# HGRN2 within a chunk: a tree of block totals, with keys and queries scaled in place level by level

## The chip, the cores and the metric

The kernel runs on one core of one Trainium2 chip. The metric is the device time of one execution in microseconds, the median of the runs; lower is better. The core has five engines that run side by side, each with an instruction queue of its own that it works through in order: PE (matrix products), DVE (elementwise work on vectors), ACT (functions such as the exponential), POOL (a second, more general elementwise engine) and SP (which here issues the DMAs).

## The reference

The reference is a two-layer decoder trunk on 512 tokens of width 1024. Layer 0 is attention, layer 1 a recurrent mixer (a Mamba-2 group and an HGRN2 group), each followed by a gated feed-forward part; a norm ends it. The change touches the HGRN2 group alone, four heads with 128 keys and 128 values each:

```python
log_f = jnp.logaddexp(jnp.log(lb), jnp.log1p(-lb) + jax.nn.log_sigmoid(xf))
k_in = (1.0 - lb) * jax.nn.sigmoid(-xf)
...
g_cum = jnp.cumsum(gc, axis=2)
decay = jnp.exp(jnp.where(causal, g_cum[:, :, :, None, :] - g_cum[:, :, None, :, :], -jnp.inf))
scores = jnp.einsum('bhlk,bhlsk,bhsk->bhls', qc, decay, kc)
o = o_inter + jnp.einsum('bhls,bhsv->bhlv', scores, vc)
```

So the score of token l against an earlier token s is a sum over 128 features of query times key times the exponential of the gates' sum from s+1 to l, a decay that differs from feature to feature. `o_inter` is what the state before the chunk adds.

## The kernel before

The work is written as Python generators whose steps are woven into one program; a scheduler then orders each engine's instructions ahead of time, from that order and from estimated durations. On the chip every queue's order is fixed.

All large products are 512 tokens wide. Weights arrive in 512-column pieces by SP's queue and are split into a high part on ACT (L292) and a low part on DVE (L294, on POOL for some early pieces); a product is three passes (L330 to L332).

`recurrent_layer` first runs the layer's projections. Then it merges five streams, `ssd` and the four calls of `hgrn_head`, which start five steps apart (`H1`), and weaves them with `recurrent_fill`, which has the remaining projections and the first parts of the output projection. When everything is through, `out_last` adds the last two heads' features (L972), with the norm of the feed-forward part in its wake.

`hgrn_head` keeps features on partitions and 512 tokens on columns, in four chunks of 128. It prepares the log of the gate, G, and the key k (L1255 to L1268). The scores in a chunk are then gathered by levels with block lengths m = 1, 2, 4, ... 64: at level m, every odd block of m queries meets the even block of m keys before it. The decay is split at the border of the two blocks: a key is scaled by the exponential of the gates' sum from it to the end of its block, a query by that from the start of its block to it. For these exponents the kernel keeps two running sums: G, which at level m holds the sum from the start of a token's block to the token, and S, the sum from the token to the end of its block. At each level from 4 on:

```python
nc.scalar.activation(out=bl(E, m)[:, :, 0, :], in_=bl(S, m)[:, :, 0, :], func=AF.Exp)
tt(out=bl(qk, m)[:, :, 0, :], in0=bl(k, m)[:, :, 0, :], in1=bl(E, m)[:, :, 0, :], op=ALU.mult)
pt(out=bl(S, m)[:, :, 0, :], in0=bl(S, m)[:, :, 0, :], in1=tot(1), op=ALU.add)
```

and the same for the queries with G (L1319, L1320, L1322). `nc.scalar` is ACT, `tt` a DVE and `pt` a POOL instruction; all are 256 columns wide, since half of the tokens are keys and half queries at a level. `qk` is a fresh buffer out of a pool of ten (`tmp`) at every level; long-lived buffers come from a pool of 37 (`slot`). PE multiplies the scaled keys with the scaled queries (L1349, blocks of 32 and 64 at L1341; levels 1 and 2 share the products of L1330, with unscaled queries for level 1 in the first half of `mv`). `keep` copies the entries that count into the score tile `sc` (L1276), one level later. After the last level the sums S and G reach over a whole chunk and give, by two more exponentials and products (L1356 to L1360), the keys and queries for the state between chunks (L1363 to L1385). The rest of a head is its norm (L425 to L429) and the split of its output (L1398, L1399).

Of the kernel before, what the change touches and what calls it, by code (L numbers as in the profile page):

```python
# [17 lines left out]
P = 128  # L18
D = 1024
T = 512  # L20
# [9 lines left out]
# in a rotated head the two halves' features lie 16 apart, in groups of 32  # L30
# [3 lines left out]
# columns of the packed per-channel parameters  # L34
# [27 lines left out]
# columns of the packed constants  # L62
# [12 lines left out]
def constants():  # L75
# [9 lines left out]
    # rows: s; compact columns: the l in odd blocks of m, in order  # L85
# [3 lines left out]
    # level 1 takes the odd l's diagonal along, the even l's stands last  # L89
# [25 lines left out]
def weave(main, fill):  # L115
    """Traces two streams of work side by side. A step is the time it stands for, or a condition to be met by the other stream."""
# [29 lines left out]
def merge(starts, cost):  # L146
    """Steps of several streams, each begun at its time, one step a unit of time."""
# [17 lines left out]
def hooked(gen, hooks):  # L165
    """The steps of gen, with calls before some of them."""
    for n, step in enumerate(gen):
        if n in hooks:
            hooks[n]()
        yield step  # L170


def begun(gen, n, cost):
    """The first n steps of gen."""
    for _ in range(n):
        next(gen)
        yield cost
# [7 lines left out]
class Build:  # L185
# [49 lines left out]
    # ---- weights: loaded ahead, split exactly into two float32r parts  # L235
    def weight_order(self):
        """Chunks in the order of their use: key, number, source, columns, columns of a piece."""
# [37 lines left out]
    def cut_one(self):  # L275
        """Splits the next piece exactly into two float32r parts."""
# [24 lines left out]
    def tick(self, now):  # L301
        """Runs the splitting ahead of piece now, where buffers are free."""
# [7 lines left out]
    def defer(self, n, f):  # L310
        """Calls f after n more steps of the projections."""
        self.waiting.append((self.ticks + n, f))
# [6 lines left out]
    def use(self, p):  # L319
        """All pieces before p have served."""  # L320
# [13 lines left out]
    def featmajor(self, ps, w, tile, ah, al, ks=None):  # L334
        """[128 features, 512 tokens] of a tile of the chunk w against the k-tiles (high, low) of the activations."""
# [18 lines left out]
    def tokmajor(self, ps, w, ah, al, b):  # L354
        """[128 tokens of block b, 512 columns]."""
# [11 lines left out]
    def tokmajor4(self, key, ah, al, evac):  # L367
        """All four blocks of a 512-wide projection."""
# [6 lines left out]
    def first_tiles(self, w, then, now=None, before=None):  # L375
        """The first two tiles of a layer, and the norm while they run; then takes them up when the norm's row is there."""
# [21 lines left out]
    # ---- norms  # L398
    def root(self, r, v, ln, f=1.0):
        """r = (f * v) ** -0.5, with a step of Newton's after the tables."""  # L400
# [7 lines left out]
    def rstd(self, acc, n, out, pre=None, post=None, by=1.0):  # L408
        """1/sqrt(mean + eps) of every token, the same row on all partitions, from the sums of squares that lie spread over
        partitions; pre: scales the sums, post and by: scale the result. Returns its second part."""  # L410
# [5 lines left out]
        def rest():  # L416
# [7 lines left out]
            # a step of Newton's after the tables  # L424
# [10 lines left out]
    def tokens(self, row):  # L435
        """A row of 512 tokens, the same on every partition, to [128 tokens, 4]."""
# [49 lines left out]
    # ---- the program  # L486
# [21 lines left out]
    def masks(self):  # L508
        """The causal masks, and the parameters that come after the first norm."""
# [15 lines left out]
    # ---- first layer: attention  # L525
# [45 lines left out]
    def rotary(self, h, c, ps):  # L571
        """Turns the queries (c = 0) or keys of head h."""
# [4 lines left out]
        # the two maps' halves: queries high over high and low, keys high and low on either half  # L577
# [148 lines left out]
    def to_features(self, ot, hi, lo, scale=None):  # L726
        """[128 tokens, 4 blocks, 128 features] to [128 features, 512 tokens], split."""
# [5 lines left out]
    def diff_attention(self):  # L733
# [17 lines left out]
        def head_end(h, oc):  # L751
            """Rms over the head, scaled by the largest magnitude so that no square overflows; where the
            plain sum of squares is beyond float32, its reciprocal root is 0."""
# [137 lines left out]
    def out_part(self, key, c, tiles, ah, al, last=False):  # L891
        """Adds some of the mixers' features through a chunk of the output projection."""
# [666 lines left out]
```

## Time and profile before

| | |
|---|---|
| runs shown | 1332.38, 1329.40, 1330.32 us; median 1330.32 |
| profiled execution, span from first to last instruction | 1328.1 us |
| median of the runs less that span | 2.2 us |
| instructions | 16545 |

The profile gives no total for the profiled execution beside its span; 2.2 us is taken for what lies around it. A row of a group of instructions names the line, the engine, the operation, the tiles written and read with partitions x columns, and the count; then busy time in us, the mean of one in ns, and the engine's idle time just before them with what ended it. Idle time that an engine spends while PE is fed costs nothing.

### The profile page before, as it was taken

The page shows a single profiled execution, that of the slowest core. Times are in us where ns is not written, and L with a number is a line of the kernel's source. Part 1 is how long each engine was busy: PE and PEld are TensorE (multiplying, and loading weights), DVE is VectorE, ACT ScalarE, POOL GpSimd, SP SyncE. Part 2 cuts the span into 40 slices and gives each one's busy share as a digit, 9 for nine tenths or more (in the row PEclk, how much of TensorE's full clock was granted, in tenths as well). Part 3 has the DMA queues.
Part 4 walks back from the last instruction along what each step waited for, and adds up shares of the span by engine and source line. Part 5 has one row for each costly group of instructions (what it writes and reads, how often), then busy time and mean ns, then how long its engine had stood idle before and what let it go on. Part 6 is the DMA issues. An engine that isn't in the chain of part 4 may idle for free.

```text
span 1328.1 us, 16545 instructions
## 1 busy us (share of the span) xinstructions
PE 1279.5 (96%) x6013; PEld 1032.1 (78%) x6013; DVE 743.1 (56%) x1298; ACT 558.7 (42%) x1119; POOL 355.6 (27%) x304
## 2 busy tenths in 40 slices
PE   7999889999999999999999999888899999999997
PEld 5766667778888888888888877676688888888886
DVE  7887885557444334444465555989954433344332
ACT  5555554445333223334443454666543322233341
POOL 2524432136222002221100014655322210122212
PEclk9998999999999999999999999999999999999998
DMA  7211221113222332223322410111122233322221
GB/s 238 95 64 32 79 65 49 48 48 112 95 86 87 110 110 100 96 66 107 113 68 92 137 66 21 65 43 54 50 109 97 78 104 111 105 95 85 82 72 64
DMA packets 37139, 112.78 MB, mean 85 GB/s; under 512 B 4273, under 2 KB 10801, under 8 KB 37057
## 3 DMA queue, kind: packets, MB, share of 16 engines
q1 hardware_dynamic: 37056, 111.72, 25.2%
q8 instruction: 48, 0.79, 0.2%
q14 instruction: 35, 0.28, 0.1%
HBM read 109.61 MB, written 2.10 MB: 84 GB/s over the span
## 4 chain that ended last, share of the span: by engine, by line
PE 79%; DVE 13%; ACT 3%; issue 2%; POOL 1%; DMA 1%; SPq 0%; POOLq 0%; DVEq 0%; ACTq 0%
PE mm L330 23%; PE mm L332 23%; PE mm L331 23%; PE o L867 2%; DVE wl L294 2%; PE at L718 1%; DVE qk L1306 1%; DVE xl L451 1%; PE at L701 1%; DVE qk L1320 1%; DVE nm L708 1%; PE at L702 0%; DMA par<-in_par_dram 0%; DMA x<-in_x_dram 0%; PE at L1349 0%
## 5 line engine op out<-in xcount | busy, mean ns | idle before, releaser
L294 DVE TENSOR_TENSOR wl<-wr,wh 128x512 fp32r<-128x512 f32 (+1 forms) x352 | 274.7, 783 | 313.2 <-ACT wh L292 311.2
L292 ACT CAST wh<-wr 128x512 fp32r<-128x512 f32 (+1 forms) x401 | 242.9, 610 | 448.3 <-PE mm L331 395.3
L330 PE MATMUL mm<-xh,wh 128*128 128x512 f32 x944 | 376.0, 399 | 7.0 <-ACT wh L292 6.4
L331 PE MATMUL mm<-xl,wh 128*128 128x512 f32 x944 | 371.5, 394 | 4.4 <-DVE xl L451 4.4
L332 PE MATMUL mm<-xh,wl 128*128 128x512 f32 x944 | 371.2, 393 | 0.0
L330 PEld LDWEIGHTS mm<-xh,wh 128*128 128x128 f32 x944 | 178.7, 189 | 48.4 <-ACT wh L292 6.3
L331 PEld LDWEIGHTS mm<-xl,wh 128*128 128x128 f32 x944 | 178.9, 190 | 42.6 <-DVE xl L451 6.7
L332 PEld LDWEIGHTS mm<-xh,wl 128*128 128x128 f32 x944 | 178.9, 190 | 37.3 <-DVE wl L294 0.2
L929 POOL TENSOR_TENSOR uu<-uu,g 128x512 f32<-128x512 f32 x44 | 69.9, 1590 | 433.1 <-DVE uu L928 409.0
L330 PE MATMUL mm<-hh,wh 128*128 128x512 f32 (+1 forms) x363 | 139.1, 383 | 0.0
L331 PE MATMUL mm<-hl,wh 128*128 128x512 f32 (+1 forms) x363 | 138.9, 383 | 0.0
L332 PE MATMUL mm<-hh,wl 128*128 128x512 f32 (+1 forms) x363 | 138.9, 383 | 0.0
L294 POOL TENSOR_TENSOR wl<-wr,wh 128x512 fp32r<-128x512 f32 (+1 forms) x54 | 70.1, 1303 | 148.7 <-ACT wh L292 148.7
L331 PEld LDWEIGHTS mm<-hl,wh 128*128 128x128 f32 x363 | 68.2, 188 | 13.4
L330 PEld LDWEIGHTS mm<-hh,wh 128*128 128x128 f32 x363 | 68.2, 188 | 13.3
L332 PEld LDWEIGHTS mm<-hh,wl 128*128 128x128 f32 x363 | 68.2, 188 | 13.2
L462 POOL TENSOR_TENSOR acc<-acc,sq 128x512 f32<-128x512 f32 x31 | 45.1, 1456 | 116.2 <-ACT sq L461 115.3
L928 DVE TENSOR_TENSOR uu<-mm,row 128x512 f32<-128x512 f32 x42 | 29.0, 691 | 65.7 <-PE mm L332 65.7
L931 POOL TENSOR_TENSOR hl<-uu,hh 128x512 fp32r<-128x512 f32 x44 | 56.5, 1287 | 29.2 <-ACT hh L930 29.2
L930 ACT CAST hh<-uu 128x512 fp32r<-128x512 f32 x44 | 27.3, 620 | 86.4 <-POOL uu L929 86.4
L710 ACT ACTIVATE p<-at,nm 128x128 f32<-128x128 f32 (+3 forms) x64 | 33.6, 526 | 49.6 <-DVE nm L708 46.1
L954 DVE TENSOR_TENSOR x<-x,mm 128x512 f32<-128x512 f32 x31 | 21.3, 687 | 36.3 <-PE mm L332 36.3
(423 smaller groups left out, 1787.3 us busy)
## 6 DMA issues: line engine op xcount, KB each, us to landing
wr<-in_w_gu_dram SPq DMA_DIRECT2D x88, 512.0 KB, 3.7
wr<-in_w_down_dram SPq DMA_DIRECT2D x32, 512.0 KB, 3.5
wr<-in_w_in_dram SPq DMA_DIRECT2D x20, 512.0 KB, 3.7
wr<-in_w_out_dram SPq DMA_DIRECT2D x12, 512.0 KB, 3.7
wr<-in_w_down_dram SPq DMA_DIRECT2D x32, 192.0 KB, 2.3
wr<-in_w_dv_dram SPq DMA_DIRECT2D x4, 512.0 KB, 4.7
tab<-in_con_dram SPq DMA_DIRECT2D x8, 256.0 KB, 4.3
wr<-in_w_z_dram SPq DMA_DIRECT2D x4, 512.0 KB, 3.4
```

The source lines that it names most:

```text
L292: nc.scalar.copy(out=hi, in_=raw)
L294: (nc.gpsimd if PL[0] <= self.cut < PL[1] else nc.vector).tensor_tensor(out=lo, in0=raw, in1=hi.bitcast(F32), op=ALU.subtract)
L330: mm(out, lh, rh, start=start, stop=False)
L331: mm(out, lh, rl, start=False, stop=False)
L332: mm(out, ll, rh, start=False, stop=stop)
L462: (nc.vector if fast else nc.gpsimd).tensor_tensor(out=acc, in0=acc, in1=t, op=ALU.add)
L710: nc.scalar.activation(out=pt[:, 0:n], in_=s[:, 0:n], func=AF.Exp, bias=nm, accum_out=rsum)
L867: nc.tensor.matmul(ops[c0 : c0 + 64, vi * P : vi * P + P], self.v[j][:, vh * 64 : (vh + 1) * 64], pT[:, j * P : (j + 1) * P], start=j == 0 ...
L928: nc.vector.tensor_tensor(out=u, in0=pu, in1=row, op=ALU.mult)
L929: nc.gpsimd.tensor_tensor(out=u, in0=u, in1=g, op=ALU.mult)
L930: nc.scalar.copy(out=h, in_=u)
L931: nc.gpsimd.tensor_tensor(out=lo, in0=u, in1=h.bitcast(F32), op=ALU.subtract)
```

## The change

Within `hgrn_head`, the running sums S and G per level are left out. The exponential of the gate of every token is taken once (E). The tree F holds the gates' totals of blocks of 2, 4, ... 128 (and 256) tokens, each level the sum of neighbouring pairs of the one below, and its exponential is taken in one instruction. Two buffers, ks and qs, are scaled for the first two levels and then, after the products of each level m, multiplied in place: keys in even blocks by the exponential of the total of the block behind them, queries in odd blocks by that of the block before. What they hold after m = 64 serves the state, and the chunk's decay is read from F. Both products of DVE are 256 columns wide. Outside `hgrn_head` only comments go. The diff, without the lines of comments:

```diff
         lv = self.lv
         yield lambda: h in self.f
         xf, q = self.f.pop(h), self.hq[h]
-        k, G, S, t1, t2 = self.slot("hk"), self.slot("G"), self.slot("S"), self.tmp("t1"), self.tmp("t2")
+        k, G, F, t1, t2 = self.slot("hk"), self.slot("G"), self.slot("F"), self.tmp("t1"), self.tmp("t2")
         nc.scalar.activation(out=t1, in_=xf, func=AF.Abs)
         nc.scalar.activation(out=t1, in_=t1, func=AF.Exp, scale=-1.0)
         nc.scalar.activation(out=t1, in_=t1, func=AF.Ln, bias=1.0)
...
         late = []
 
         def keep(n, m, ps, part):
 
             def f():
                 nc.vector.copy_predicated(
...
         for c in range(4):
             nc.tensor.matmul(even[:, c, :], k[:, c * P : (c + 1) * P], bl(q, 1)[:, c * 64 : (c + 1) * 64, 0, :], start=True, stop=True)
         keep(7, 1, even, 0)
-        kd, mv, E = self.tmp("qk"), self.tmp("mv"), self.tmp("E")
-        nc.scalar.activation(out=E[:, 0:256], in_=bl(G, 1)[:, :, 1, 0], func=AF.Exp)
-        tt(out=bl(kd, 1)[:, :, 0, 0], in0=bl(k, 1)[:, :, 0, 0], in1=E[:, 0:256], op=ALU.mult)
-        nc.scalar.copy(out=bl(kd, 1)[:, :, 1, 0], in_=bl(k, 1)[:, :, 1, 0])
+        at = lambda m: T - 2 * T // m
+        E, mv = self.tmp("E"), self.tmp("mv")
+        nc.scalar.activation(out=E, in_=G, func=AF.Exp)
         nc.scalar.copy(out=chunk(mv)[:, :, 0:64], in_=chunk(q)[:, :, 1::2])
-        nc.gpsimd.tensor_copy(out=bl(S, 1)[:, :, 0, :], in_=bl(G, 1)[:, :, 1, :])
-        nc.gpsimd.memset(bl(S, 1)[:, :, 1, :], 0.0)
-        pt(out=bl(G, 1)[:, :, 1, :], in0=bl(G, 1)[:, :, 1, :], in1=bl(G, 1)[:, :, 0, :], op=ALU.add)
+        src = G
+        for m in LEVELS:
+            pair = src.rearrange("p (b two) -> p b two", two=2)
+            out = F[:, at(2 * m) : at(2 * m) + T // (2 * m)]
+            tt(out=out, in0=pair[:, :, 0], in1=pair[:, :, 1], op=ALU.add)
+            src = out
+        nc.scalar.activation(out=F[:, 0 : at(256)], in_=F[:, 0 : at(256)], func=AF.Exp)
+        ks, qs = self.slot("ks"), self.slot("qs")
+        tt(out=bl(ks, 1)[:, :, 0, 0], in0=bl(k, 1)[:, :, 0, 0], in1=bl(E, 1)[:, :, 1, 0], op=ALU.mult)
+        nc.scalar.copy(out=bl(ks, 1)[:, :, 1, 0], in_=bl(k, 1)[:, :, 1, 0])
+        tt(out=bl(qs, 1)[:, :, 0, 0], in0=bl(q, 1)[:, :, 0, 0], in1=bl(E, 1)[:, :, 0, 0], op=ALU.mult)
+        tt(out=bl(qs, 1)[:, :, 1, 0], in0=bl(q, 1)[:, :, 1, 0], in1=F[:, 0:256], op=ALU.mult)
+        nc.scalar.copy(out=chunk(mv)[:, :, 64:128].rearrange("p c (b m) -> p c b m", m=2), in_=bl(qs, 2)[:, :, 1, :].rearrange("p (c b) m -> p c b m", c=4))
         yield 860
         for n, m in list(enumerate(LEVELS))[1:]:
-            nb = T // (2 * m)
-            tot = lambda i: bl(G, m)[:, :, i, m - 1 : m].broadcast_to([P, nb, m])
-            if m > 2:
-                qk, E = self.tmp("qk"), self.tmp("E")
-                nc.scalar.activation(out=bl(E, m)[:, :, 0, :], in_=bl(S, m)[:, :, 0, :], func=AF.Exp)
-                tt(out=bl(qk, m)[:, :, 0, :], in0=bl(k, m)[:, :, 0, :], in1=bl(E, m)[:, :, 0, :], op=ALU.mult)
-            if m <= 64:
-                pt(out=bl(S, m)[:, :, 0, :], in0=bl(S, m)[:, :, 0, :], in1=tot(1), op=ALU.add)
-            if m == 2:
-                nc.scalar.activation(out=bl(E, 256)[:, 0, 1, :].rearrange("p (b m) -> p b m", m=2), in_=bl(G, 2)[:, :, 1, :], func=AF.Exp)
-                pairs = lambda t: t.rearrange("p c (b m) -> p c b m", m=2)
-                tt(
-                    out=pairs(chunk(mv)[:, :, 64:128]),
-                    in0=bl(q, 2)[:, :, 1, :].rearrange("p (c b) m -> p c b m", c=4),
-                    in1=pairs(chunk(E[:, 256:T])),
-                    op=ALU.mult,
-                )
-            else:
-                nc.scalar.activation(out=bl(E, m)[:, :, 1, :], in_=bl(G, m)[:, :, 1, :], func=AF.Exp)
-                tt(out=bl(qk, m)[:, :, 1, :], in0=bl(q, m)[:, :, 1, :], in1=bl(E, m)[:, :, 1, :], op=ALU.mult)
-            if m <= 64:
-                pt(out=bl(G, m)[:, :, 1, :], in0=bl(G, m)[:, :, 1, :], in1=tot(0), op=ALU.add)
             for f in late:
                 f()
             late.clear()
...
                 ps = self.bank("at")
             if m == 2:
                 for c in range(4):
-                    nc.tensor.matmul(ps[:, c * P : (c + 1) * P], kd[:, c * P : (c + 1) * P], mv[:, c * P : (c + 1) * P], start=True, stop=True)
+                    nc.tensor.matmul(ps[:, c * P : (c + 1) * P], ks[:, c * P : (c + 1) * P], mv[:, c * P : (c + 1) * P], start=True, stop=True)
                 keep(0, 1, chunk(ps)[:, :, 0:64], 1)
                 keep(1, 2, chunk(ps)[:, :, 64:128], 1)
                 yield 860
             elif m in (32, 64):
                 part = chunk(ps[:, 256 * (n % 2) : 256 * (n % 2) + 4 * m])
                 blocks = range(0, P, 2 * m)
                 for c in range(4):
                     for b in blocks:
                         t = c * P + b
-                        nc.tensor.matmul(part[b : b + m, c, :], qk[:, t : t + m], qk[:, t + m : t + 2 * m], start=True, stop=True)
+                        nc.tensor.matmul(part[b : b + m, c, :], ks[:, t : t + m], qs[:, t + m : t + 2 * m], start=True, stop=True)
                 for b in blocks:
                     late.append(lambda b=b, m=m, part=part: HC(nc)(out=chunk(sc)[b : b + m, :, b + m : b + 2 * m], in_=part[b : b + m]))
                 yield 500
-            elif m <= 64:
+            else:
                 half = ps[:, 256 * (n % 2) : 256 * (n % 2) + 256]
                 for c in range(4):
-                    odd = bl(qk, m)[:, c * (64 // m) : (c + 1) * (64 // m), 1, :]
-                    nc.tensor.matmul(half[:, c * 64 : c * 64 + 64], qk[:, c * P : (c + 1) * P], odd, start=True, stop=True)
+                    odd = bl(qs, m)[:, c * (64 // m) : (c + 1) * (64 // m), 1, :]
+                    nc.tensor.matmul(half[:, c * 64 : c * 64 + 64], ks[:, c * P : (c + 1) * P], odd, start=True, stop=True)
                 keep(n, m, chunk(half), 1)
                 yield 860
+            nb = T // (2 * m)
+            both = F[:, at(m) : at(m) + 2 * nb].rearrange("p (b two) -> p b two", two=2)
+            for t, i in ((ks, 0), (qs, 1)):
+                tt(out=bl(t, m)[:, :, i, :], in0=bl(t, m)[:, :, i, :], in1=both[:, :, 1 - i].unsqueeze(2).broadcast_to([P, nb, m]), op=ALU.mult)
         for f in late:
             f()
-        kd, qd, E = self.tmp("kd"), self.tmp("qd"), self.tmp("E")
-        nc.scalar.activation(out=E[:, 0:384], in_=S[:, 0:384], func=AF.Exp)
-        tt(out=kd[:, 0:384], in0=k[:, 0:384], in1=E[:, 0:384], op=ALU.mult)
-        EG = self.tmp("EG")
-        nc.scalar.activation(out=EG[:, P:T], in_=G[:, P:T], func=AF.Exp)
-        tt(out=qd[:, P:T], in0=q[:, P:T], in1=EG[:, P:T], op=ALU.mult)
+        kd, qd, EG = ks, qs, F[:, at(128) : at(128) + 4]
         ps, kt = self.bank("at"), self.tmp("kt")
         for c in range(3):
             nc.tensor.transpose(ps[:, c * P : (c + 1) * P], kd[:, c * P : (c + 1) * P], self.ident)
...
         nc.vector.tensor_copy(out=state(0), in_=ps[:, 0:P])
         for c in (1, 2):
             nc.vector.scalar_tensor_tensor(
-                out=state(c), in0=state(c - 1), scalar=EG[:, c * P + 127 : c * P + 128], in1=ps[:, c * P : (c + 1) * P], op0=ALU.mult, op1=ALU.add
+                out=state(c), in0=state(c - 1), scalar=EG[:, c : c + 1], in1=ps[:, c * P : (c + 1) * P], op0=ALU.mult, op1=ALU.add
             )
         yield 660
         o = self.bank("o")
...
```

## Rows read from the trace of the kernel before

**Rows 1.** The page, part 1: busy us, share of the span, instructions

```profile
PE 1279.5 (96%) x6013; PEld 1032.1 (78%) x6013; DVE 743.1 (56%) x1298; ACT 558.7 (42%) x1119; POOL 355.6 (27%) x304
```

**Rows 2.** Busy us of PE, PEld, DVE, ACT, POOL by stretch; then PE clock, DMA

```profile
826.00:935.00 109.00, 95.66 (x611) 77.68 (x610) 98.59 (x178) 67.23 (x159) 66.43 (x77) 1.00 0.15 49
...
700.00:760.00 60.00, 60.00 (x268) 49.68 (x267) 30.44 (x58) 23.68 (x38) 0.00 (x0) 1.00 0.32 109
```

**Rows 3.** PE's waits from 826 to 944 us: total us, times, longest

```profile
PE at L1349 <- DVE qk L1320: 5.1, 6, 1.4
PE at L1341 <- DVE qk L1320: 4.8, 5, 1.5
...
PE at L1330 <- DVE mv L1312: 0.8, 2, 0.5
```

**Rows 4.** DVE groups from 826 to 935 us: busy us, mean ns | idle before

```profile
L294 DVE TENSOR_TENSOR wl<-wr,wh 128x512 fp32r<-128x512 f32 x22 | 17.5, 804 | 0.7 <-ACT wh L292 0.7
L1306 DVE TENSOR_TENSOR qk<-hk,E 128x256 f32<-128x256 f32 x20 | 15.8, 791 | 0.4
L1320 DVE TENSOR_TENSOR qk<-hq,E 128x256 f32<-128x256 f32 x20 | 13.5, 675 | 0.4 <-ACT E L1319 0.4
L1276 DVE COPY_PREDICATED sc<-lv,at 128x256 f32<-128x256 uint8 x23 | 13.2, 575 | 2.9 <-PE at L1349 1.2 <-PE at L1288 1.1 <-PE at L1330 0.6
...
L1360 DVE TENSOR_TENSOR qd<-hq,EG 128x384 f32<-128x384 f32 x4 | 3.3, 834 | 0.0
...
L1312 DVE TENSOR_TENSOR mv<-hq,E 128x256 f32<-128x256 f32 x4 | 2.5, 621 | 0.0
...
L1293 DVE TENSOR_TENSOR qk<-hk,E 128x256 f32<-128x256 f32 x4 | 2.3, 581 | 1.7 <-ACT E L1292 1.7
...
L1357 DVE TENSOR_TENSOR kd<-hk,E 128x384 f32<-128x384 f32 x4 | 2.2, 547 | 0.0
...
L1374 DVE COPY st<-at 128x128 f32<-128x128 f32 x4 | 1.1, 285 | 0.0
...
L404 DVE TENSOR_TENSOR yln<-yri 128x1 f32<-128x1 f32 x3 | 0.5, 177 | 0.5 <-ACT yri L403 0.5
```

**Rows 5.** POOL groups from 818 to 950 us

```profile
L1308 POOL TENSOR_TENSOR S<-S,G 128x256 f32<-128x256 f32 x24 | 20.4, 852 | 18.4 <-ACT E L1305 17.6
L1322 POOL TENSOR_TENSOR G<-G 128x256 f32<-128x256 f32 x24 | 19.8, 830 | 1.6 <-ACT E L1319 0.2
...
L1298 POOL TENSOR_TENSOR G<-G 128x256 f32<-128x256 f32 x4 | 3.5, 865 | 0.3
...
L1296 POOL COPY S<-G 128x256 f32<-128x256 f32 x4 | 2.3, 574 | 0.2
```

**Rows 6.** ACT groups from 818 to 950 us

```profile
L1305 ACT ACTIVATE E<-S 128x256 f32<-128x256 f32 x20 | 8.3, 414 | 1.9 <-POOL S L1308 1.8
...
L1359 ACT ACTIVATE EG<-G 128x384 f32<-128x384 f32 x4 | 2.1, 519 | 0.0
```

**Rows 7.** Single lines: ns shortest/median/longest; L294 from 700 to 760 us

```profile
L1306 DVE TENSOR_TENSOR qk<-hk,E x20: 425/840/1297, 830.5 to 926.2; 128x256 f32<-128x256 f32 x20
...
L1276 DVE COPY_PREDICATED sc<-lv,at x23: 416/449/758, 833.8 to 923.4; 128x256 f32<-128x256 uint8 x23
...
L294 DVE TENSOR_TENSOR wl<-wr,wh x24: 681/692/693, 701.9 to 757.9; 128x512 fp32r<-128x512 f32 x24
```

**Rows 8.** Order of time, POOL and DVE near 844 us: start, us

```profile
843.73 1.30 POOL L1268 TENSOR_TENSOR G<-G,t 128x512 f32<-128x512 f32 x1
...
844.13 1.18 DVE L1306 TENSOR_TENSOR qk<-hk,E 128x256 f32<-128x256 f32 x1
```

**Rows 9.** Order of time, PE, head 0's first level groups: start, us

```profile
832.97 1.00 PE L1349 MATMUL at<-qk 128*128 128x64 f32 x8
...
836.29 1.10 PE L1349 MATMUL at<-qk 128*128 128x64 f32 x8 [1.17 <-DVE yri L406]
```

## The prediction

> **What bounds the kernel now.** I read the busy shares first, then a table of busy time by stretch, then PE's waits, then the groups of instructions on DVE, POOL and ACT in the one stretch that the change touches, and at last single instructions there.
>
> Over the whole span PE is busy 96%, DVE 56% and POOL 27% [rows 1]: a kernel bound by its products, where an engine beside PE matters only where PE waits for it. The table by stretch says where that is. From 826 to 935 us, where the four HGRN2 heads run, DVE is busy 98.6 of 109 us, PE 95.7, POOL 66.4; between 700 and 760 us, in the feed-forward part, PE has no idle time, DVE has half of its own free, and POOL does nothing [rows 2]. So in the heads' stretch DVE is full, and PE has 13.3 us without work (109.0 - 95.7) at a granted clock of 1.00. PE's waits name the cause: 5.1 + 4.8 + 0.8 = 10.7 us for DVE's products of keys and queries with their decay, L1320 and L1312 [rows 3], which is 80% of the 13.3. What stands after this stretch is fed by PE alone, so what is saved or lost here reaches the end of the kernel nearly whole.
>
> What fills DVE: per head, twelve products of 256 columns (L1293, L1312, five each of L1306 and L1320) and two of 384 (L1357, L1360); in all 15.8 + 13.5 + 2.5 + 2.3 + 2.2 + 3.3 = 39.6 us, beside the weights' low parts (L294, 17.5) and the predicated copies (L1276, 13.2) [rows 4]. They are slower than they need be. The same 256-column product takes 425 ns at its shortest and 1297 at its longest, and L294, at 804 ns here, takes 681 to 693 where POOL is idle [rows 4, 7]. The longer ones stand beside POOL: L1306 at 844.13 took 1.18 us, and for most of it POOL's L1268 was running, from 843.73 to 845.03 [rows 8]. What POOL does meanwhile is above all the running sums that the change removes [rows 5].
>
> **The change, part by part.** The sums are against the profiled execution: span 1328.1 us, and 2.2 us around it up to the median of 1330.3.
>
> *POOL.* Per head the copy (L1296), the first sum (L1298) and twelve sums (L1308, L1322) go, and a memset. Without the memset that is 20.4 + 19.8 + 3.5 + 2.3 = 46.0 us [rows 5] of 66.4: 31% of POOL's time stays (20.4 us).
>
> *DVE, removed.* The 39.6 us above, fourteen instructions per head.
>
> *DVE, added.* Per head twenty-two: fifteen products of 256 columns (three that start the scaled keys and queries, two after each of six levels) and a tree of seven sums with 256, 128, 64, 32, 16, 8 and 4 columns. No row has these small sums; the nearest are 285 ns for 128 columns (L1374) and about 170 for one (L404) [rows 4]; I take 0.29 for the second sum, 0.18 for each of the five last, 1.2 us together, which the two rows hold between 0.9 and 1.7. For the sixteen of 256 columns the lower end is the shortest seen, 0.42 us [rows 7], and the upper end today's mean, (15.8 + 13.5 + 2.5 + 2.3) / 48 = 0.71 [rows 4]. With 31% of POOL left, and the excess of 0.29 in proportion, one costs 0.42 + 0.31 x 0.29 = 0.51. So the added work is 4 x (16 x 0.51 + 1.2) = 37.4 us, at the lower end 31.7, at the upper 50.2.
>
> *DVE, relieved.* L294 could fall from 804 to 692 ns, 22 times, 2.5 us; L1276 from 575 to its 416, 23 times, 3.7 us [rows 4, 7]: 6.2 us if POOL no longer disturbs, 4.3 in proportion.
>
> So DVE's sum changes by -39.6 + 37.4 - 4.3 = -6.5 us in proportion, by -39.6 + 31.7 - 6.2 = -14.1 if all its instructions run undisturbed, and by +10.6 if nothing is relieved. I take the middle of the first two, -10.3: much of what POOL keeps (the gate's preparation, the low part of a head's output) lies at a head's ends, not among the levels.
>
> The Trainium skill, "SBUF — State Buffer", section "Who interferes with whom", states that a VectorE instruction with two inputs in SBUF and a GpSimd instruction that reads SBUF shut each other out for a whole instruction. By this rule the excess is all POOL's and vanishes with it, so that the sum would lie at its undisturbed end, -14.1; the proportional reading of the rows gives -6.5. The trace agrees with the rule in kind (1.18 us against 0.42 for the same product), and no row here shows the levels without POOL.
>
> *ACT.* Ten exponentials of 256 columns at 0.41 us (L1305, and L1319 like it), two more of 256 and two of 384 at 0.52 go per head; two of about 512 and a copy of 256 columns come [rows 6]. ACT is busy 67 of 109 us [rows 2]; I count nothing for it. If ACT's order put something in front of a split of weights, it could cost a fraction of a microsecond.
>
> *The first level comes later.* Before, a POOL sum (0.87, L1298), an exponential (0.41) and a product (0.62) stand between a head's gate and the second product of the level pair [rows 4 to 6]; now the tree (0.51 + 1.2), an exponential of 508 columns (from 0.52 for 384, an estimate of 0.63), a product (0.51) and ACT's copy (about 0.41, as L1305): 3.3 in place of 1.9 us, 1.4 per head. PE's cover is the projections' products and the other heads; I count 0.2 per head, 0.8 us, and 5.6 if that cover is gone.
>
> *In place.* Keys and queries were written into a fresh buffer at each level; now level n+1 may be written only when the products of level n have been read. That is a new wait of DVE for PE, with the other heads' products, the weights' low parts and PE's next level queued behind it. Two products at 0.42 to 0.51, PE's group of about 1.0 and the two handovers make some 2.1 us per level of one head. Head 0's first two groups of L1349 start 3.3 us apart, 832.97 and 836.29 [rows 9]. So I count nothing; if it is exposed, it is the first rival. PE's instructions and the DMAs keep their number, and SP's queue is not touched. Of the kernel's buffers, three new ones per head (F, ks, qs) come for S, and some fifteen temporary ones go; G and k are free after the first level.
>
> *Head's end.* The exponentials and products of 384 columns before the states go (in the sums above); the last level's two products are the scaled keys and queries.
>
> **Sum.** DVE's -10.3 us reach PE to 80%, the share of its idle time that waits for these products: -8.3, and +0.8 for the later start: -7.5. Span 1320.6, time 1322.8 us. The best end is all of PE's idle time in the stretch, 13.3 us, 1317.0, and somewhat less if the norm behind it also meets an emptier DVE: 1315.
>
> **Rivals.**
> 1. *The in-place chain is exposed (slower).* At each of 24 level steps PE finds nothing between a level's products and the next one's, and waits for two DVE products and a handover, about 0.95 us: 22.8 us, where it waits 10.7 now. That is +12.1, 1342 us. It decides once less than 0.95 us of other PE work stands between two levels of a head. For it: PE runs its queue in order, so a planned gap can't be filled later, and 10.7 us of such waits exist already. Against it: 3.3 us between levels, and up to three heads beside the projections. 10%.
> 2. *DVE gets no relief (slower).* If the excess is not POOL's doing, the sixteen cost 0.71 and DVE has +10.6 us where it is full: 1341 us. Against it stand L294's two durations and the instruction at 844.13 [rows 7, 8]. 6%. A second way to that side is a price per instruction that width does not lower: eight more per head at L404's 0.17 us [rows 4] are 4 x 1.4 = 5.4 us, 1336; of the 6% this has 2. The Trainium skill, "VectorE: DVE Perf Modes", section "Rules for kernel authors", says to keep the number of chained VectorE instructions small, since each of them drains the pipe; that speaks against going from fourteen to twenty-two.
> 3. *The waits stay (no change).* PE's queue is fixed ahead; if the new order asks for the products as early as the old one does, DVE's free time turns into its own waiting for PE, and PE waits as before: the gain is given back to the later start and to DVE's new waits, 1328 to 1332 us. For it: DVE has 10.4 us idle in the stretch already, while PE waits. 14%.
>
> **How the numbers follow.** The forecast has 70%, 1315 to 1327.6. A measurement of this kernel tells about 0.2%, 2.7 us, from no change. So faster (under 1327.7) 0.70, same (to 1333.0) 0.14, slower 0.16. The likeliest time is 1322.8; the range from 1315 to 1332 holds the forecast's cases and most of the third rival, and leaves out the two slower ones.
>
> **What would show it.** Right: POOL's busy time between the heads' first and last product falls to about 20 us, DVE's 256-column products to about 0.42 to 0.55 us, the exponentials go from fourteen to two per head, PE's waits for DVE's keys and queries fall below some 4 us, and the stretch of 109 us is 7 to 8 us shorter with PE's busy time unchanged. Wrong: DVE's products still at 0.7 us (rival 2); long waits of PE for the in-place products, with DVE waiting for PE's level products between them (rival 1); the same PE waits with an emptier DVE (rival 3); or the gap moves to the heads' starts, where PE waits for the copy into the moving operand.

## The result, and the profile after

| | before | after |
|---|---|---|
| median of the runs | 1330.92 us | 1315.28 us |
| ratio, 95% interval | | 0.9896 [0.9874, 0.9919] |
| span of the profiled execution | 1328.1 us | 1313.0 us |
| from the first HGRN2 instruction (L1255) to the feed-forward part's first product | 131.4 us | 119.0 us |

The kernel is faster by 1.04%; measured a second time, beside other kernels, by 0.79% (0.9921 [0.9900, 0.9942], median 1319.1 us where 1313 to 1318 was expected). Every ratio here is against the kernel before on the same chip, whose median lies between 1328.7 and 1330.9 us. Runs of one kernel can lie 5 us apart (the second time 1313.8, 1318.9, 1319.4 and 1319.6), so the totals don't tell a microsecond or two between two kernels. The traces tell more, but each is of one execution; where that one lies more than 1.5 us off its kernel's median, the text says so.

First the span's busy shares, after. [rows 1] is the line of before:

```profile
PE 1274.8 (97%) x6013; PEld 1029.9 (78%) x6013; DVE 732.2 (56%) x1330; ACT 545.5 (42%) x1075; POOL 308.2 (23%) x244
```

DVE has 32 instructions more (eight per head) and 10.9 us less to do; POOL lost 47.4 us, ACT 13.2. PE has the same 6013 products. Where the time went is seen in one stretch with the same PE work in both kernels, from head 0's first instruction to the feed-forward part's first product. The columns are those of [rows 2]: length, then PE, PEld, DVE, ACT, POOL, and the granted clock, which is the share of PE's full clock that it was given. Before, then after:

```profile
818.82:950.18 131.36, 117.28 (x711) 94.98 (x710) 115.94 (x210) 80.22 (x181) 72.28 (x84) 1.00 0.15 49
```

```profile
817.22:936.19 118.97, 115.75 (x711) 95.50 (x711) 106.50 (x243) 67.12 (x138) 24.52 (x24) 1.00 0.17 54
```

Of the span's 15.1 us, 12.4 are here: PE's idle time falls from 14.1 to 3.2 us (length less busy), and PE's busy time by 1.5: the durations of its products add up to the same (231.1 and 231.2 us), but they overlap more. The rest isn't put down to the change: 1.6 us lie before the first head's instruction, a point that varies from 816.3 to 822.4 us over the traces shown here though no code ahead of it was changed, and 1.1 behind the stretch. DVE's busy time falls by 9.4 us. PE's waits in the stretch, after (compare [rows 3]):

```profile
PE at L1337 <- DVE ks L1343: 0.9, 1, 0.9
...
PE at L1329 <- DVE qs L1343: 0.5, 1, 0.5
PE at L1318 <- ACT mv L1308: 0.3, 1, 0.3
```

Of the 10.7 us for the products of keys and queries, 1.7 are left. DVE's groups, after, from 818 to 921 us, where the heads run, answer to [rows 4]:

```profile
L294 DVE TENSOR_TENSOR wl<-wr,wh 128x512 fp32r<-128x512 f32 x21 | 15.3, 728 | 0.0
L1276 DVE COPY_PREDICATED sc<-lv,at 128x256 f32<-128x256 uint8 x24 | 13.8, 574 | 3.1 <-PE at L1288 3.1
L1343 DVE TENSOR_TENSOR qs<-qs,F 128x256 f32<-128x256 f32 x24 | 12.4, 517 | 0.0
L1343 DVE TENSOR_TENSOR ks<-ks,F 128x256 f32<-128x256 f32 x24 | 11.6, 485 | 3.1 <-PE at L1337 1.7 <-PE at L1329 1.1 <-PE at L1318 0.3
...
L1299 DVE TENSOR_TENSOR F<-G 128x256 f32<-128x256 f32 x4 | 1.7, 418 | 1.8 <-POOL G L1268 1.8
...
L1299 DVE TENSOR_TENSOR F<-F 128x64 f32<-128x64 f32 x4 | 0.9, 213 | 0.0
...
L1299 DVE TENSOR_TENSOR F<-F 128x4 f32<-128x4 f32 x4 | 0.6, 148 | 0.0
```

The in-place products take 0.50 us where their forerunners took 0.73 (791 and 675 ns), the weights' low parts 728 ns instead of 804 (over the whole stretch, 761 instead of 790). The predicated copies have not changed, 574 against 575.

These means mix two kinds. Counted one by one in the trace of before, 42 of the 48 products of 256 columns (L1293, L1306, L1312, L1320) overlap in time with an instruction of POOL that reads, and take 754 ns on the mean; the other six take 407 to 412. In the changed kernel 12 of 60 have such a neighbour, with a mean of 755, and the other 48 take 404 to 453. So the excess stands beside POOL's reading instructions and nowhere else.

### The profile page after: what moved, and what is told of

Its sections match the earlier page's. It is cut to its first block, busy times and chain, and to the rows that moved or that the text cites. A ratio compares the mean times of both kernels' runs of the same rounds, so it can differ in the third digit from the quotient of the medians.

```text
span 1313.0 us, 16410 instructions
## 1 busy us (share of the span) xinstructions
PE 1274.8 (97%) x6013; PEld 1029.9 (78%) x6013; DVE 732.2 (56%) x1330; ACT 545.5 (42%) x1075; POOL 308.2 (23%) x244
## 4 chain that ended last, share of the span: by engine, by line
PE 83%; DVE 10%; ACT 2%; issue 1%; DMA 1%; POOL 1%; SPq 0%; POOLq 0%; DVEq 0%; ACTq 0%
PE mm L330 24%; PE mm L331 24%; PE mm L332 24%; PE o L867 2%; PE at L718 1%; DVE wl L294 1%; PE at L1337 1%; DVE xl L451 1%; PE at L701 1%; DVE nm L708 1%; DMA x<-in_x_dram 0%; PE at L702 0%; DMA par<-in_par_dram 0%; PE at L332 0%; PE at L330 0%
## 5 line engine op out<-in xcount | busy, mean ns | idle before, releaser
L294 DVE TENSOR_TENSOR wl<-wr,wh 128x512 fp32r<-128x512 f32 (+1 forms) x352 | 272.8, 777 | 312.2 <-ACT wh L292 310.1
L294 POOL TENSOR_TENSOR wl<-wr,wh 128x512 fp32r<-128x512 f32 (+1 forms) x54 | 70.1, 1303 | 147.4 <-ACT wh L292 147.4
L331 PEld LDWEIGHTS mm<-hl,wh 128*128 128x128 f32 x363 | 68.2, 188 | 13.4
L332 PEld LDWEIGHTS mm<-hh,wl 128*128 128x128 f32 x363 | 68.2, 188 | 13.2
```

What stands on the lines that cost most here:

```text
L294: (nc.gpsimd if PL[0] <= self.cut < PL[1] else nc.vector).tensor_tensor(out=lo, in0=raw, in1=hi.bitcast(F32), op=ALU.subtract)
L331: mm(out, lh, rl, start=False, stop=False)
L332: mm(out, ll, rh, start=False, stop=stop)
```

## The experiments

Three theories stood at the start. A: POOL's running sums stretch DVE's instructions, and DVE's work bounds the stretch. B: the chain from a sum on POOL over an exponential on ACT to DVE's product made PE wait, whatever the durations. C: the change's own fewer exponentials and other products bring the gain. "The stretch" is the one above in every kernel. Kernels named b come from the kernel before, those named a from the changed one.

### Running sums left out (b_nosum), and run for nobody (b_free)

In both, all fourteen exponentials of a head read t1, which is finished before the levels and is kept in a long-lived buffer; the first pair of lines stands for them. In b_nosum the sums go too, and with them L1296 to L1298:

```diff
-nc.scalar.activation(out=bl(E, m)[:, :, 0, :], in_=bl(S, m)[:, :, 0, :], func=AF.Exp)
+nc.scalar.activation(out=bl(E, m)[:, :, 0, :], in_=bl(t1, m)[:, :, 0, :], func=AF.Exp)
...
-pt(out=bl(S, m)[:, :, 0, :], in0=bl(S, m)[:, :, 0, :], in1=tot(1), op=ALU.add)
-pt(out=bl(G, m)[:, :, 1, :], in0=bl(G, m)[:, :, 1, :], in1=tot(0), op=ALU.add)
```

> The kernel before, with POOL's running sums left out (its copy, memset and thirteen sums per head) and every exponential of the levels reading the same finished tile, so that the output is not the reference's. Exponentials, DVE products and PE's work keep their number and widths. Theory A (POOL's instructions stretch DVE's): DVE's 256-column products fall from about 0.71 to 0.42 to 0.50 us, 10 us of DVE's work go, and the time is 1317 to 1322 us. Theory B (the chain sum, exponential, product before each level made PE wait): about the same, 1316 to 1321, but also if the products keep their length. Theory C (the fewer and other products of the change bring the gain): no change, 1329 to 1332.

> The same, but POOL runs all its running sums; nothing reads them. Theory A (stretch): the products stay near 0.7 us, time 1327 to 1332, the kernel before's. Theory B (chain): the products may start early whatever POOL does, PE's waits for DVE's products fall from 10.7 to under 4 us, time 1316 to 1322. Theory C: 1329 to 1332.

Measured: b_nosum 1316.5 us, 0.9905 [0.9886, 0.9924]; b_free 1338.0 us, 1.0061 [1.0038, 1.0084]. Without the sums, the two groups of products (query, key) and the stretch:

```profile
L1315 DVE TENSOR_TENSOR qk<-hq,E 128x256 f32<-128x256 f32 x20 | 9.5, 474 | 0.1
L1303 DVE TENSOR_TENSOR qk<-hk,E 128x256 f32<-128x256 f32 x20 | 9.4, 472 | 0.2 <-ACT E L1302 0.2
```

```profile
816.75:937.53 120.78, 116.15 (x713) 95.33 (x712) 104.71 (x210) 79.11 (x183) 23.50 (x24) 1.00 0.17 53
```

This kernel has all fourteen exponentials and fourteen products per head (ACT 79 us, as before) and is as fast as the changed one. That ends theory C: the gain comes with POOL's sums gone, and the tree is what allows that. B fails on b_free: no exponential waits for a sum, and it is slower, not faster; it is slower than A allowed for, too (1327 to 1332). Its stretch (the trace is of the slowest of four runs, 1344.0 us), and two lines that show how far the sums reach, the product at a head's end and PE's longest wait:

```profile
822.44:963.23 140.79, 121.93 (x713) 98.54 (x712) 119.22 (x210) 79.75 (x183) 69.57 (x84) 0.96 0.15 46
```

```profile
L1357 DVE TENSOR_TENSOR kd<-hk,E 128x384 f32<-128x384 f32 x4 | 3.5, 872 | 0.0
```

```profile
PE at L1349 <- DVE yri L406: 5.8, 1, 5.8
```

Freed of the exponentials, POOL runs the sums of a head in one burst. The products fare better than before (645 and 638 ns against 791 and 675), but other DVE work that falls into a burst fares worse: L1357 takes 872 ns where [rows 4] has 547. So this run can't separate the sums' cost from their placement; the next one does.

### The pace kept, the chain cut (b_paced), and half of it (b_half)

Against b_free; b_half has only the first of the two new lines, and no sum of G at the levels:

```diff
-pt(out=bl(S, m)[:, :, 0, :], in0=bl(S, m)[:, :, 0, :], in1=tot(1), op=ALU.add)
+pt(out=bl(S, m)[:, :, 0, :], in0=bl(E if m > 2 else S, m)[:, :, 0, :], in1=tot(1), op=ALU.add)
-pt(out=bl(G, m)[:, :, 1, :], in0=bl(G, m)[:, :, 1, :], in1=tot(0), op=ALU.add)
+pt(out=bl(G, m)[:, :, 1, :], in0=bl(E if m > 2 else G, m)[:, :, 1, :], in1=tot(0), op=ALU.add)
```

> The kernel before with the chain cut but the pace kept: the exponentials read a finished tile, and each running sum of POOL from level 4 on reads the exponential of its level, so that the sums come spread over the levels as before and no exponential waits for one. The output is not the reference's. Theory A (POOL's instructions stretch DVE's): products near 0.7 us, PE's waits near 10 us, time 1327 to 1333, as before. Theory B (the chain of sums before each level): time 1316 to 1322.

> The paced kernel before with a cut chain, with the 24 sums S kept and the 28 of G left out, so that about half of POOL's disturbing time stays. The output is not the reference's. If PE's loss goes with the stretched DVE time: products near 0.58 us and a time half way between 1332 and 1316, 1321 to 1327. If PE's waits vanish as soon as DVE isn't full (a threshold, which would explain that more was won than DVE was relieved by): 1315 to 1320. If any sum of POOL brings the waits back: 1328 to 1333.

Measured: b_paced 1332.3 us, 1.0031 [1.0016, 1.0045]; b_half 1326.4 us, 0.9985 [0.9972, 0.9998]. Stretch and products of b_paced (the trace is of its fastest run, 1329.8 us):

```profile
816.28:950.88 134.60, 120.61 (x713) 97.78 (x712) 121.65 (x210) 79.75 (x183) 69.56 (x84) 0.97 0.15 48
```

```profile
L1306 DVE TENSOR_TENSOR qk<-hk,E 128x256 f32<-128x256 f32 x20 | 15.6, 780 | 0.0
L1320 DVE TENSOR_TENSOR qk<-hq,E 128x256 f32<-128x256 f32 x20 | 14.0, 700 | 0.0
```

The durations are those of before, and so is the time, a little worse, with no exponential waiting for a sum. That ends B. PE's idle time in the stretch is as before, 14.0 us; what is longer is its busy time, at a granted clock of 0.97 where before had 1.00. Of b_half:

```profile
817.99:948.22 130.23, 118.73 (x713) 96.65 (x712) 114.44 (x210) 79.49 (x183) 49.52 (x60) 0.99 0.15 49
```

```profile
L1306 DVE TENSOR_TENSOR qk<-hk,E 128x256 f32<-128x256 f32 x20 | 14.0, 699 | 0.0
L1320 DVE TENSOR_TENSOR qk<-hq,E 128x256 f32<-128x256 f32 x20 | 11.2, 561 | 0.0
```

With 28 of the 52 sums left (the 24 S and, in L1298, the four that start G), the mean product takes 0.63 us, and the time lies between the two ends, nearer to the slow one. At this half the waits have not vanished at once.

### The sums put back beside the tree (a_sums), and fills in their place (a_memset)

Per level, on two tiles D and S that nothing else uses, `tot` being that of the kernel before, of D; first a_sums, then a_memset. At a head's start a_sums has two fills and one sum more, a_memset three fills:

```diff
+pt(out=bl(S, m)[:, :, 0, :], in0=bl(S, m)[:, :, 0, :], in1=tot(1), op=ALU.add)
+pt(out=bl(D, m)[:, :, 1, :], in0=bl(D, m)[:, :, 1, :], in1=tot(0), op=ALU.add)
```

```diff
+nc.gpsimd.memset(S, 0.0)
+nc.gpsimd.memset(S, 0.0)
+nc.gpsimd.memset(D, 0.0)
```

> The changed kernel with POOL's running sums put back on two tiles of zeros that nothing reads (two memsets and thirteen sums of 256 columns per head). Theory A (stretch): the in-place products go from about 0.50 to 0.65 to 0.75 us, DVE has some 10 us more, time 1322 to 1328. Theory B (chain): nothing waits for the sums, time 1314 to 1317 as with the change. Theory C: 1314 to 1317.

> The changed kernel with POOL filling two spare tiles with zeros where the run before put running sums: per head 21 fills of 512 columns, about 0.52 us each, some 11 us that read nothing. If any POOL instruction stretches DVE's, time 1325 to 1342, as with the sums. If only POOL instructions that read do (theory A in the form of the shared read port), 1314 to 1318, and the 64-column sum of the tree stays at about 0.21 us.

Measured: a_sums 1341.7 us, 1.0104 [1.0080, 1.0129]; a_memset 1315.2 us, 0.9891 [0.9872, 0.9910]. The stretch of a_sums, two of the tree's sums, and PE's two longest waits:

```profile
817.09:960.97 143.88, 126.15 (x712) 102.69 (x711) 124.18 (x243) 67.45 (x138) 71.86 (x84) 0.93 0.14 45
```

```profile
L1299 DVE TENSOR_TENSOR F<-F 128x64 f32<-128x64 f32 x4 | 3.1, 782 | 0.0
...
L1299 DVE TENSOR_TENSOR F<-F 128x4 f32<-128x4 f32 x4 | 1.5, 384 | 0.0
```

```profile
PE at L1325 <- ACT mv L1312: 6.0, 3, 3.4
PE mm L331 <- DVE yl L451: 3.4, 1, 3.4
```

The direction is A's and the size is beyond it. The sums came in a burst at each head's start, as in b_free, and fell on the tree: its sum of 64 columns takes 782 ns for 213, and the tree holds up the first level of its head. The in-place products lengthen little on the mean (529 and 543 ns), because 26 of the 48 have no reading instruction of POOL beside them (420 ns); the other 22 take 673. DVE's busy time grows by 17.7 us and the stretch by 24.9: PE's idle time is 17.7 us against 3.2, and its busy time 10.4 us longer at a granted clock of 0.93 against 1.00. The stretch of a_memset, its fills and the tree beside them:

```profile
816.41:936.15 119.74, 115.92 (x711) 95.49 (x711) 107.23 (x243) 67.20 (x138) 65.33 (x108) 1.00 0.17 54
```

```profile
L1314 POOL MEMSET S<- 128x512 f32 x24 | 12.8, 531 | 0.5
```

```profile
L1299 DVE TENSOR_TENSOR F<-F x24: 147/177/295, 825.8 to 895.7; 128x128 f32<-128x128 f32 x4, 128x64 f32<-128x64 f32 x4, 128x32 f32<-128x32 f32 x4, 128x16 f32<-128x16 f32 x4
```

POOL is nearly as busy as in a_sums (65.3 against 71.9 us), and nothing is lost. All 28 sums of the tree run beside a fill, and the 18 in-place products that have fills alone beside them take 407 to 464 ns. So it is not POOL's being busy that hurts; a fill differs from a sum in that it reads nothing. This agrees with the Trainium skill, "SBUF — State Buffer", section "Who interferes with whom", which excepts GpSimd instructions that only write.

### The in-place chain loosened (a_loose)

```diff
- tt(out=bl(t, m)[:, :, i, :], in0=bl(t, m)[:, :, i, :], in1=..., op=ALU.mult)
+ tt(out=bl(self.tmp("w"), m)[:, :, i, :], in0=bl(t, m)[:, :, i, :], in1=..., op=ALU.mult)
```

> The changed kernel with the two products per level written to a spare tile instead of in place, so that later levels read unscaled keys and queries: the output is not the reference's. Same instructions, but no product waits for PE and no level of PE waits for a product. If the in-place wait is hidden, as I counted it: 1313 to 1317, as with the change. If it is exposed (rival 1 of the prediction, in part): PE's last 3 us of idle time in the heads' stretch go, 1309 to 1313.

Measured: 1314.6 us, 0.9895 [0.9875, 0.9915], against 0.9896 with the chain.

```profile
819.65:939.23 119.58, 115.12 (x711) 95.76 (x711) 107.65 (x243) 67.11 (x138) 25.05 (x24) 1.00 0.17 54
```

The wait that writing in place adds costs nothing that can be seen; the trace is of the slowest of its four runs (1317.4 us), and its stretch is 0.6 us longer than the changed kernel's.

### More DVE work with a quiet POOL (a_dve)

Once per level, ahead of the two products in place, with E kept in a long-lived buffer:

```diff
+W = self.tmp("w")
+tt(out=bl(W, m)[:, :, 0, :], in0=bl(E, m)[:, :, 0, :], in1=both[:, :, 1].unsqueeze(2).broadcast_to([P, nb, m]), op=ALU.mult)
```

> The changed kernel with one more DVE product of 256 columns per level and head, of tiles that are there, into a spare tile: 24 more, 10 to 12 us of DVE's time, with POOL left quiet. If DVE's sum is what the stretch goes by: 1322 to 1328. If DVE's 12 us of idle time take it up and only stretched instructions hurt: 1314 to 1318.

Measured: 1328.9 us, 1.0000 [0.9979, 1.0021], beside 0.9921 for the changed kernel on the same chip.

```profile
816.58:946.64 130.06, 117.98 (x711) 97.47 (x710) 114.96 (x267) 67.82 (x138) 27.30 (x24) 0.97 0.15 49
```

```profile
L1343 DVE TENSOR_TENSOR w<-E,F 128x256 f32<-128x256 f32 x24 | 11.4, 480 | 0.0
```

```profile
PE at L1329 <- DVE qs L1345: 6.3, 3, 3.6
```

Twenty-four products that nobody reads, 11.4 us, give back the whole gain by the medians; the trace, of one of the fastest of ten runs (1324.3 us, the others up to 1334.6), has a stretch 11.1 us longer than the changed kernel's and 1.3 us shorter than that of before. With about the same busy time of DVE as before (115.0 against 115.9 us) the stretch is about as long, though here the time goes into work and there into contention. So DVE's busy time sets this stretch's length, to a first approximation. One rival stays: the added product stands ahead of the two in place, so it also lengthens each level's own step, and no run tells the two apart.

### The tree on POOL (a_treepool), a head's start on DVE (a_gdve)

First a_treepool, then a_gdve:

```diff
-tt(out=out, in0=pair[:, :, 0], in1=pair[:, :, 1], op=ALU.add)
+pt(out=out, in0=pair[:, :, 0], in1=pair[:, :, 1], op=ALU.add)
```

```diff
-pt(out=t2, in0=t1, in1=xf, op=ALU.subtract)
+tt(out=t2, in0=t1, in1=xf, op=ALU.subtract)
...
-pt(out=G, in0=G, in1=t1, op=ALU.add)
+tt(out=G, in0=G, in1=t1, op=ALU.add)
```

> The changed kernel with the tree's seven sums on POOL in place of DVE. DVE has 6.3 us less in the heads' stretch, POOL seven short instructions per head more. If DVE's work still bounds the stretch: 1312 to 1314. If PE's 3 us of idle time there leave nothing to win: 1314 to 1317. If the later start of a head counts (the prediction's 1.4 us per head, uncovered, here with slower sums) or the short sums stretch DVE: 1317 to 1322.

> The changed kernel with POOL's two 512-column instructions of a head's start (1.37 and 1.32 us) on DVE, at about 0.68 each: DVE has 5.5 us more, POOL 10.8 less, and a head starts up to 1.3 us earlier. If POOL's last reading instructions still stretch DVE's, or a head's start counts: 1311 to 1314. If DVE's sum counts: 1317 to 1321. If neither: 1314 to 1317.

Measured: a_treepool 1327.2 us, 0.9975 [0.9959, 0.9991], worse than any expectation; a_gdve 1316.1 us, 0.9902 [0.9886, 0.9919], not told apart from the change (0.9921 beside it). The stretch of a_treepool (a run of 1328.8 us, the others from 1322.2 to 1330.3), two pieces of it, PE's longest wait, and one of the tree's sums on POOL:

```profile
825.00:835.00 10.00, 7.83 (x42) 6.58 (x41) 5.47 (x13) 6.02 (x15) 4.75 (x10) 0.91 0.01 2
835.00:845.00 10.00, 10.00 (x49) 8.68 (x49) 6.38 (x17) 4.58 (x8) 1.27 (x1) 0.75 0.00 0
...
817.85:950.22 132.37, 122.15 (x711) 101.83 (x710) 103.37 (x215) 67.77 (x138) 36.44 (x52) 0.94 0.15 49
```

```profile
PE at L1318 <- ACT mv L1308: 5.3, 3, 2.7
```

```profile
L1299 POOL TENSOR_TENSOR F<-F 128x64 f32<-128x64 f32 x4 | 1.4, 355 | 0.3
```

DVE has the least work of all kernels here, 103.4 us, and the stretch is 132.4 us long, so DVE's busy time is not the only thing that can set it. The tree's chain on POOL is slower (the 64-column sum 355 ns, for 213 on DVE), the first level's products come late, and PE waits for `mv`. Behind such a gap the granted clock is 0.75 in the next 10 us, part of the time at the lower of its two levels, and the mean over the stretch 0.94. So a head's start is on PE's path when it is slow enough, which it isn't with the tree on DVE (0.3 us of waits for `mv`). Of the 13.4 us by which the stretch is longer than the changed kernel's, 7.0 are idle time of PE (10.2 against 3.2) and 6.4 its busy time on the same 711 products (122.2 against 115.8), at the lower clock. In a_gdve DVE's busy time grows by 0.6 us only (107.1 against 106.5), not by the 5.5 that were expected.

### The norm's sums on DVE (a_accdve)

```diff
-(nc.vector if fast else nc.gpsimd).tensor_tensor(out=acc, in0=acc, in1=t, op=ALU.add)
+(nc.vector if fast or self.wcol == C_NFFN + 8 else nc.gpsimd).tensor_tensor(out=acc, in0=acc, in1=t, op=ALU.add)
```

> The changed kernel with the sums of squares of the norm behind the mixer (seven of 512 columns, 1.64 us each on POOL) on DVE instead, beside the low parts that PE waits for there. If POOL stretches those low parts (about 1.16 us where 0.68 is the undisturbed time): they fall to 0.7 us, but DVE gets seven instructions of 0.7 us: 1313 to 1316. If DVE's queue is the bound there: 1316 to 1319.

Measured: 1313.6 us, 0.9891 [0.9863, 0.9919]: the same as the change. The low parts of the norm's output, from 930 to 960 us, in the changed kernel and here:

```profile
L451 DVE SCALAR_TENSOR_TENSOR xl<-x,par,xh 128x512 fp32r<-128x512 f32 x8 | 9.3, 1164 | 0.0
```

```profile
L451 DVE SCALAR_TENSOR_TENSOR xl<-x,par,xh 128x512 fp32r<-128x512 f32 x8 | 5.9, 743 | 0.0
```

They fall from 1164 to 743 ns, as expected, 3.4 us in all, and DVE gets seven sums of 0.68 us, 4.8 us. No version tried here beats the changed kernel by more than its interval.

## Why the prediction was right, and where not

The time lies in the range, on the side forecast, but at its lower end: 15.6 us were won where 7.5 were forecast, and the median is 0.3 us inside the range. That it is inside at all is in part luck: 15.1 us of it are in the profiled spans, and of these only 12.4 in the stretch that the forecast spoke of.

*POOL.* 46.0 us removed were expected, and a memset that was left uncounted; POOL's time in the stretch fell by 47.8 (72.3 to 24.5). The share that stays was put at 31%, but that sets sums from 818 to 950 us against a busy time from 826 to 935; over one stretch it is 34% (24.5 of 72.3).

*DVE.* -10.3 us were expected, between the proportional -6.5 and the undisturbed -14.1, and its busy time fell by 9.4. These two aren't the same measure. The forecast added up durations of instructions. Added up like that, DVE's durations in the stretch fall from 131.2 to 124.7 us, by 6.5, the proportional figure: from 39.6 to 35.3 for the removed and added instructions, and by 2.2 for all others. In the trace an instruction of DVE mostly starts some 0.08 us before the one ahead of it has ended (in the changed kernel the sum of 32 columns runs from 848.09 to 848.27 us, and the copy behind it starts at 848.19). Busy time counts that overlap once, so 33 instructions more, many of them short, add less to it than to the sum of durations. So that -9.4 is near -10.3 is luck. By its parts: the in-place products cost 0.50 us as taken (0.51), the three that start a head 0.41; the tree 1.58 us (418 ns for its first sum, 282, 213, 179, 178, 157 and 148), estimated 0.51 + 1.2. The relief of L1276 (up to 3.7 us) did not come: 574 ns after 575. Its 416 ns at the shortest was not the undisturbed mean that I took it for. L294 gained 76 of the 112 ns that it could while the heads run, and 29 over the whole stretch.

*The step that failed* is "DVE's -10.3 us reach PE to 80%, the share of its idle time that waits for these products". By busy time they reached it to 130% (12.4 for 9.4). What PE gained in the stretch has three parts: its waits for the products of keys and queries fell by 9.0 us (10.7 to 1.7), the later start counted in, 1.5 more than the 7.5 that were forecast; its other idle time fell too, by 1.9 us (3.4 to 1.5); and its own products overlap more, 1.5 us. The last two stand in no term of the sum. The clock has no part in it: 1.00 in both. The remaining 3.2 us of the 15.6 are the 2.7 outside the stretch and 0.5 between the profiled spans and the medians, and no run ties them to the change. What DVE's busy time is worth can be read from the stretches of all kernels:

| kernel | DVE busy, us | stretch, us | PE idle, us | granted clock |
|---|---|---|---|---|
| a_treepool | 103.4 | 132.4 | 10.2 | 0.94 |
| b_nosum | 104.7 | 120.8 | 4.6 | 1.00 |
| after | 106.5 | 119.0 | 3.2 | 1.00 |
| a_accdve | 106.5 | 119.0 | 3.3 | 1.00 |
| after, again (1313.8 us, the fastest of four) | 106.6 | 119.0 | 3.2 | 1.00 |
| a_gdve | 107.1 | 120.6 | 4.4 | 0.99 |
| a_memset | 107.2 | 119.7 | 3.8 | 1.00 |
| a_loose | 107.7 | 119.6 | 4.5 | 1.00 |
| b_half | 114.4 | 130.2 | 11.5 | 0.99 |
| a_dve | 115.0 | 130.1 | 12.1 | 0.97 |
| before | 115.9 | 131.4 | 14.1 | 1.00 |
| b_free | 119.2 | 140.8 | 18.9 | 0.96 |
| b_paced | 121.7 | 134.6 | 14.0 | 0.97 |
| a_sums | 124.2 | 143.9 | 17.7 | 0.93 |

From before to after it is 12.4 us for 9.4, from after to a_dve 11.1 for 8.5, from before to b_nosum 10.6 for 11.2: about one for one. It is no constant: from before to b_paced 3.2 us for 5.7, to b_free 9.4 for 3.3, and a_treepool, whose DVE has the least to do, waits for its slow tree. DVE was 88% busy in the stretch before and 90% after, so its idle time fell together with its work (15.4 to 12.5 us); why was not tested. The share of PE's waits that a view ascribes to one line is no factor for what comes back: here waits that it ascribes to other lines shrank as well. Of all of PE's idle time, which the prediction named as the best end, 3.2 us are left.

*The later start.* 0.8 us was counted, and 0.3 us of PE's waits for `mv` is seen. That the cover can go is shown by a_treepool (5.3 us).

*In place.* Rightly counted at nothing (a_loose). *ACT*, counted at nothing: rightly, since b_nosum keeps every exponential and is as fast.

*Rivals.* The exposed chain did not occur: PE's waits for the in-place products are 1.4 us. "No relief" fell with the durations. Its second form, a price per instruction, is there in kind, since the sum of 4 columns still takes 148 ns, but the tree's 1.2 us had it already. The count rose from fourteen to twenty-two per head, and their durations fell from 39.6 to 35.3 us, since each costs less. This is against the direction of the Trainium skill's rule from "VectorE: DVE Perf Modes", section "Rules for kernel authors", to keep chained instructions few. Beside a reading POOL the count would have weighed more: in a_sums the tree takes 15.7 us in place of 6.3. "The waits stay" was wrong in its premise that the order of PE's queue keeps them: PE's idle time fell by 10.9 us with the same 711 products.

## What to carry to other kernels

An engine that is nearly full over one stretch (here 88%) can set its length, though it is 56% busy over the span; then a microsecond of its busy time is worth roughly one of the kernel's, whichever line the waits are ascribed to. A simple test is to add work that nobody reads, off the chain that you want to leave alone. Where many instructions are short, count an engine's busy time over a window and not the sum of its durations. Before you offload sums from DVE to POOL, look at what they do to DVE's durations: work on POOL that reads is not free, and doing it on DVE in another form can be cheaper than the contention. Keep a chain of short instructions that a stage's first product waits for on the engine with the short instruction.

## What the runs showed that was not expected

- In these runs contention does not cost a wide instruction more than a narrow one. Beside POOL's back-to-back sums in a_sums a DVE sum of 64 columns takes 782 ns for 213 and one of 4 columns 384 for 148, 0.57 and 0.24 us more; the 22 in-place products of 256 columns that overlap with a reading instruction of POOL take 673 for 420, 0.25 more.
- POOL busy 65 us, most of it with fills, costs DVE next to nothing (107.2 against 106.5 us busy); 72 us with sums costs it 17.7 us.
- The sums run for nobody cost 0.61% over before in a burst (b_free, [1.0038, 1.0084]) and 0.31% spread over the levels (b_paced, [1.0016, 1.0045]). The intervals overlap, so that the burst is dearer is not shown by these two; where it meets the tree it is 1.04% (a_sums).
- The granted clock fell behind some of PE's gaps: it is 0.75 in the 10 us after a piece with 2.2 us of idle time (a_treepool), part of that at the lower of its two levels, and 0.97 over a stretch with 14.0 us of idle time in waits of up to 2.1 us (b_paced); before, with 14.1 us in waits of up to 1.5 us, and the changed kernel have 1.00.
